# The first loads of a fused matmul-GELU-matmul in smaller pieces

## The chip, the core and the metric

The kernel runs on one core of a Trainium2 chip. The metric is the device time of one execution in microseconds; the median of several runs counts. A profile is one execution recorded by the hardware profiler, with the start and length of each instruction on TensorE (PE; its weight loads PEld), VectorE (DVE), ScalarE (ACT), GpSimd (POOL) and SyncE (SP), and the DMA packets.

## What is computed

```python
def setup_inputs():
    m, k, n, p = 1024, 1024, 2048, 1024
    # a: [m, k], b: [k, n], c: [n, p], all float32, standard normal

def reference(a, b, c):
    h = np.matmul(a, b)
    h = 0.5 * h * (1 + np.tanh(np.sqrt(2 / np.pi) * (h + 0.044715 * h ** 3)))
    return np.matmul(h, c).astype(np.float32)
```

## The kernel before

All matmuls run on 128 x 128 weights against up to 512 columns. The hidden matrix h is made transposed: its 2048 columns are 16 tiles of 128 partitions, and the 1024 rows of A are two halves (h = 0, 1 in the code) of 512. The contraction of the first product has 1024 entries, eight slices of 128 (k = 0 to 7), and pairs of slices are called quarters (q = 0 to 3). A has to lie with the contraction on the partitions, so each 128 x 128 block of it is cast to bf16, transposed on TensorE into a PSUM bank (`pt`) and copied by VectorE into `aT`.

The kernel has three stages in this order:

1. The first four column tiles of h (columns 0 to 511 of B) with plain matmuls: `block(h, tiles, ks)` adds the slices `ks` to the accumulators `ps[h, t]` of the given tiles; `gelu` writes the finished ones into `hT`. In this stage A is turned, slice by slice, in between the blocks.
2. The other column tiles, by a scheme with seven products in place of eight (`zero`, a block of 512 columns, then `one`, the last 1024), with sums and differences of operands made by VectorE.
3. The second product with C (`two`), by the same scheme, with the stores of the result.

The order on every engine is the order in which the program is written (`manual_schedule`); engines wait for each other only through tiles. The order in front is written out by hand: `stir` keeps TensorE busy with products of zeros, `cast_a` and `cast_b` cast what came in float32, `turn` transposes a quarter (two slices, with a `yield` after each), `block` does the matmuls.

Loads take two ways. SyncE's queue brings float32 into staging tiles: `sta` for A (lines 75, 77, 78: quarter 0 of both halves and quarter 1 of half 0, 512 KB each, rows of 256 columns) and `stb` for B (lines 76 and 79: slices 0 and 1 in one load of 512 KB, slice 2 of 256 KB). VectorE and ScalarE cast these. GpSimd's queue, called the casting queue here, casts on the way: `abq` for A (line 86) and straight into `b1`, `b2` and `c_sb` for B and C (lines 89, 92, 98, 101, 104). A one-column copy on GpSimd, `gate` (line 81), stands ahead of the casting loads and waits for the first load of A, so that the casting queue starts only then. The casting loads in order are: A (h=1, q=1), B slice 3, A (0,2), B slices 4 and 5, A (1,2), A (0,3), B slices 6 and 7, A (1,3), then the second column block of B, the last 1024 columns of B, and C.

Which slices of the casting queue arrive when decides what stage 1 can do: `block(0, range(4), (k,))` needs `b1[:, k]` and `aT[:, 0, k]`, and `turn(1, 3, ...)` on the last load of A stands near the end of the stage. After that stage 2 begins with products over the second column block of B.

Of the kernel before, what the change touches and what calls it, by code (L numbers as in the profile page):

```python
# [9 lines left out]
F32 = mybir.dt.float32  # L10
F32R = mybir.dt.float32r
BF16 = mybir.dt.bfloat16
# [7 lines left out]
def kernel(ctx, tc, a, b, c, out):  # L20
    nc = tc.nc
    M, K = a.shape
    _, N = b.shape
    _, P = c.shape
    H = 512
# [3 lines left out]
    av = a.rearrange("(mt p) k -> p mt k", p=128)  # L29
    bv = b.rearrange("(kt p) n -> p kt n", p=128)  # L30
# [9 lines left out]
    def slot(tag, shape, dt, name):  # L40
        return big.tile(shape, dt, name=name, tag=tag)

    def bank(i, shape=(128, H), dt=F32, name="ps"):
        return pp.tile(list(shape), dt, name=name, tag=f"bank{i}", padded_shape=None)

    def pieces(tag, bufs, shape, dt, name):
        return small.tile(shape, dt, name=name, tag=tag, bufs=bufs)

    warm = nc.const_aps.tensor(0.0, [128, 256], F32)
    ident = consts.tile([128, 128], BF16, name="ident")  # L50
    make_identity(nc, ident)
    gate = consts.tile([128, 1], F32, name="gate")
# [6 lines left out]
    aT = slot("a", [128, 2, KT, H], BF16, "aT")  # L59
    b1 = slot("b1", [128, KT, 1024], BF16, "b1")  # L60
# [2 lines left out]

    KH = KT // 2
    stb = slot("x0", [128, KT, H], F32, "stb")
    sta = slot("x1", [128, 2, 2, 4, 256], F32, "sta")
    abq = slot("x3", [128, 4, 2, 4, 256], BF16, "abq")

    def a_part(h, q):
        return av[:, 4 * h:4 * h + 4, ds(q * 256, 256)]  # L70

    def b_part(q):
        return bv[:, 2 * q:2 * q + 2, 0:H]

    nc.sync.dma_start(out=sta[:, 0, 0], in_=a_part(0, 0))
    nc.sync.dma_start(out=stb[:, 0:2], in_=b_part(0))
    nc.sync.dma_start(out=sta[:, 1, 0], in_=a_part(1, 0))
    nc.sync.dma_start(out=sta[:, 0, 1], in_=a_part(0, 1))
    nc.sync.dma_start(out=stb[:, 2], in_=bv[:, 2, 0:H])

    nc.gpsimd.tensor_copy(gate, sta[:, 0, 0, 3, 0:1])  # L81
    nc.scalar.activation(g, warm[:, 0:1], AF.Gelu_apprx_tanh)


    def cast_load_a(h, q):
        nc.gpsimd.dma_start(out=abq[:, q, h], in_=a_part(h, q))  # L86

    def cast_load_b(q):
        nc.gpsimd.dma_start(out=b1[:, 2 * q:2 * q + 2, 0:H], in_=b_part(q))  # L89

    cast_load_a(1, 1)
    nc.gpsimd.dma_start(out=b1[:, 3, 0:H], in_=bv[:, 3, 0:H])  # L92
    for q in range(2, 4):
# [5 lines left out]
    for n in range(2):  # L99
        for k in range(0, KT, 4):  # L100
            nc.gpsimd.dma_start(out=b2[:, k:k + 4, ts(n, H)],
                                in_=bv[:, k:k + 4, ds(1024 + n * H, H)])
# [3 lines left out]
    def copy(eng, dst, src):  # L106
        if eng is nc.scalar:
            nc.scalar.activation(dst, src, AF.Copy)
        else:
            nc.vector.tensor_copy(dst, src)  # L110

    def mm1(p, t, h, ks):
        for k in ks:
            nc.tensor.matmul(p, b1[:, k, ts(t, 128)], aT[:, h, k],  # L114
                             start=(k == 0), stop=(k == KT - 1))
# [6 lines left out]
    def stir(*widths):  # L122

        for w in widths:
            nc.tensor.matmul(ps[0, 3][:, 0:w], warm[:, 0:128], warm[:, 0:w],
                             start=True, stop=True, skip_group_check=True)

    def cast_a(h, q, *engs):

        ab = pieces("ab", 2, [128, 4, 256], BF16, "ab")  # L130
        for i, eng in enumerate(engs):
            w = 256 // len(engs)
            for j, e in enumerate(eng if isinstance(eng, tuple) else (eng,)):
                m = slice(2 * j, 2 * j + 2) if isinstance(eng, tuple) else slice(0, 4)
                copy(e, ab[:, m, ts(i, w)], sta[:, h, q][:, m, ts(i, w)])
        return ab

    def turn(h, q, i, ab):

        banks = i if isinstance(i, tuple) else (i,)  # L140
        pts = [bank(x, (128, 2, H), BF16, "pt") for x in banks]
        for n in range(2):
            pt = pts[n % len(pts)]
            for m in range(4):
                nc.tensor.transpose(pt[:, n, ts(m, 128)], ab[:, m, ts(n, 128)], ident)  # L145
            nc.vector.tensor_copy(aT[:, h, 2 * q + n], pt[:, n])  # L146
            yield

    def cast_b(k, *engs):
        c0 = 0  # L150
        for i, eng in enumerate(engs):
            w = (H - c0) if i == len(engs) - 1 else H // len(engs) // 128 * 128
            copy(eng, b1[:, k, ds(c0, w)], stb[:, k, ds(c0, w)])
            c0 += w

    def block(h, tiles, ks):
        for k in ks:
            for t in tiles:
                mm1(ps[h, t], t, h, (k,))
# [66 lines left out]
    zero = Seven(4, quarters(b1, H, 256), BB, [None] * 4, [None] * 4, 2)  # L226
    one = Seven(4, quarters(b2, 0, H), BB, [None] * 4, zero.t)

    stir(256, 256, 256, 256, 256)
    tn = turn(0, 0, 4, cast_a(0, 0, nc.vector))  # L230
    next(tn)
    stir(128)
    cast_b(0, nc.vector, nc.vector, nc.scalar)
    next(tn)
    stir(64)
    cast_b(1, nc.scalar)
    ab = cast_a(1, 0, nc.vector, nc.scalar)
    block(0, range(4), (0,))
    block(0, range(2), (1,))
    for _ in turn(1, 0, (7, 6), ab):  # L240
        pass
    block(0, range(2, 4), (1,))
    ab = cast_a(0, 1, (nc.scalar, nc.vector), nc.vector)
    cast_b(2, nc.scalar, nc.scalar)
    for t in range(3):
        ps[1, t] = bank(4 + t)
    zero.t[0], zero.t[1] = pair(2)
    block(1, range(3), (0,))
    tn = turn(0, 1, 7, ab)
    next(tn)  # L250
    block(1, range(3), (1,))
    next(tn)
# [1 line left out]
    for q in range(1, 3):  # L254
        k = 2 * q
        block(0, range(4), (k,))
        tn = turn(1, q, 7, abq[:, q, 1])
# [5 lines left out]
        tn = turn(0, q + 1, 7, abq[:, q + 1, 0])  # L263
# [10 lines left out]
    tn = turn(1, 3, 0, abq[:, 3, 1])  # L274
# [213 lines left out]
```

## Time and profile before

| what | us |
|---|---|
| median of 3 runs | 117.2 (117.19 to 117.28) |
| the profiled execution's own time | 117.6 |
| its span, first to last instruction | 115.8 |
| first load of A landed, GpSimd's gate starts | 4.49 |
| first matmul of the first product | 6.90 |
| last casting load of A landed | 21.58 |
| last matmul ended | 112.9 |

Granted TensorE clock 1.000 of full speed. The DMA issues of the front, from the page (line, engine, operation, count, KB each, median us from issue to landing):

```profile
b<-in_b_dram POOLq DMA_DIRECT2D x6, 512.0 KB, 15.6
sta<-in_a_dram SPq DMA_DIRECT2D x3, 512.0 KB, 6.2
abq<-in_a_dram POOLq DMA_DIRECT2D x5, 256.0 KB, 8.0
stb<-in_b_dram SPq DMA_DIRECT2D x1, 512.0 KB, 5.4
b<-in_b_dram POOLq DMA_DIRECT2D x2, 256.0 KB, 8.3
stb<-in_b_dram SPq DMA_DIRECT2D x1, 256.0 KB, 7.2
```

KB are those written: a casting load of A of 256 KB reads 512 KB. The time to landing holds the waiting in line behind earlier loads. A share of the DMA engines over 100% means that packets overlap. In the lines of a timeline the bracket tells how long the engine stood idle before the instruction, and what ended that.

### The profile page before, as it was taken

How to read it: one execution, taken by the hardware profiler on the slowest of the kernel's cores; microseconds unless marked ns; L12 is line 12 of the kernel's file. 1: busy time of each engine (PE TensorE's matmuls, PEld its weight loads, DVE VectorE, ACT ScalarE, POOL GpSimd, SP SyncE). 2: the span in 40 equal slices, each digit the busy share in tenths (PEclk: the TensorE clock that was granted, in tenths of full speed). 3: DMA queues.
4: the chain of work that ended last, by engine and by line, in shares of the span. 5: the costliest groups of instructions: out<-in, count | busy, mean ns of one | idle time of the engine just before them, and what ended most of it. 6: DMA issues, size and time to landing. Idle time of an engine off the chain costs nothing.

```text
span 115.8 us, 1473 instructions
## 1 busy us (share of the span) xinstructions
PE 110.7 (96%) x544; PEld 77.1 (67%) x550; DVE 90.1 (78%) x108; ACT 51.4 (44%) x86; POOL 17.3 (15%) x29
## 2 busy tenths in 40 slices
PE   7889999999999999999999999999999999999990
PEld 6545555445777447888886444588888888888870
DVE  0247747689999998944789999999999986964581
ACT  5053000799268998066699339700043992000000
POOL 2497754222332000000000000000000000000000
PEclk9999999999999999999999999999999999999999
DMA  3999999999999999998000000070000002004994
GB/s 74 296 381 221 200 199 204 204 207 207 205 210 210 211 212 212 212 210 163 9 0 0 6 0 0 0 272 0 0 0 0 0 0 94 2 27 173 364 358 166
DMA packets 13414, 15.94 MB, mean 138 GB/s; under 512 B 736, under 2 KB 9184, under 8 KB 13408
## 3 DMA queue, kind: packets, MB, share of 16 engines
q0 software_dynamic: 8672, 9.31, 47.6%
q1 hardware_dynamic: 4592, 6.42, 15.7%
q10 hardware_dynamic: 144, 0.13, 0.3%
q8 instruction: 4, 0.07, 0.2%
q14 instruction: 2, 0.02, 0.0%
HBM read 20.97 MB, written 4.19 MB: 217 GB/s over the span
## 4 chain that ended last, share of the span: by engine, by line
PE 79%; DMA 13%; POOL 5%; issue 0%; DVE 0%
PE ps L212 76%; DMA abq<-in_a_dram 10%; DMA sta<-in_a_dram 3%; POOL abq L86 3%; PE ps L114 2%; POOL b L89 1%; POOL gate L81 1%; PE pt L145 1%; POOL b L92 0%; DVE ot L375 0%
## 5 line engine op out<-in xcount | busy, mean ns | idle before, releaser
L212 PE MATMUL ps<-x,s 128*128 128x512 f32 x128 | 29.6, 391 | 0.0
L212 PEld LDWEIGHTS ps<-x,s 128*128 128x128 f32 x128 | 24.0, 188 | 5.1
L212 PE MATMUL ps<-x,x 128*128 128x512 f32 x96 | 22.9, 394 | 0.0
L212 PEld LDWEIGHTS ps<-x,x 128*128 128x128 f32 x96 | 18.0, 188 | 3.9
L114 PE MATMUL ps<-aT,b 128*128 128x512 bf16 x62 | 15.7, 379 | 0.3 <-DVE b L110 0.2
L298 ACT ACTIVATE v<-ps 128x512 f32<-128x512 f32 x10 | 6.0, 598 | 19.1 <-PE ps L212 19.1
L212 PE MATMUL ps<-c_sb,hT 128*128 128x512 bf16 (+2 forms) x78 | 14.1, 336 | 0.1
L212 PE MATMUL ps<-x 128*128 128x512 f32 x56 | 13.2, 393 | 0.0
L212 PEld LDWEIGHTS ps<-x 128*128 128x128 f32 x56 | 10.2, 188 | 2.7 <-ACT u L298 0.4
L212 PEld LDWEIGHTS <-hT 128*128 128x128 bf16 x80 | 7.1, 98 | 7.0 <-issue 0.5
L118 ACT ACTIVATE hT<-ps 128x512 bf16<-128x512 f32 x14 | 7.3, 596 | 9.6 <-PE ps L114 9.6
L118 ACT ACTIVATE hT<-ot 128x512 bf16<-128x512 f32 x18 | 10.4, 623 | 2.1 <-DVE ot L303 2.0
L146 DVE COPY aT<-pt 128x512 bf16<-128x512 bf16 x16 | 6.7, 422 | 5.5 <-PE pt L145 5.4
L212 PE MATMUL ps<-aT,b 128*128 128x512 bf16 x46 | 10.6, 379 | 0.1
L303 DVE TENSOR_TENSOR ot<-ps,u 128x512 f32<-128x512 f32 x10 | 6.7, 688 | 5.2 <-ACT u L298 5.2
L303 DVE TENSOR_TENSOR ot<-ps,v 128x512 f32<-128x512 f32 x10 | 6.7, 688 | 4.9 <-DMA out_dram<-ot 3.9
L170 DVE TENSOR_TENSOR x<-c_sb 128x1024 fp32r<-128x1024 bf16 x8 | 9.2, 1216 | 0.0
L114 PEld LDWEIGHTS <-b 128*128 128x128 bf16 x64 | 5.7, 97 | 4.5 <-DVE b L110 0.3
L212 PEld LDWEIGHTS <-b 128*128 128x128 bf16 x48 | 4.6, 97 | 5.7 <-issue 0.3
L104 POOL DMA_DIRECT2D c_sb<-in_c_dram x8 | 5.6, 703 | 13.4 <-DMA b<-in_b_dram 11.1
L170 DVE TENSOR_TENSOR x<-b 128x1024 fp32r<-128x1024 bf16 (+1 forms) x4 | 7.0, 1751 | 0.6 <-issue 0.6
L298 ACT ACTIVATE u<-ps 128x512 f32<-128x512 f32 x10 | 5.9, 597 | 3.4 <-PE ps L212 3.2
(44 smaller groups left out, 110.7 us busy)
## 6 DMA issues: line engine op xcount, KB each, us to landing
c_sb<-in_c_dram POOLq DMA_DIRECT2D x8, 512.0 KB, 19.7
out_dram<-ot SPq DMA_DIRECT2D x14, 256.0 KB, 2.1
b<-in_b_dram POOLq DMA_DIRECT2D x6, 512.0 KB, 15.6
sta<-in_a_dram SPq DMA_DIRECT2D x3, 512.0 KB, 6.2
abq<-in_a_dram POOLq DMA_DIRECT2D x5, 256.0 KB, 8.0
stb<-in_b_dram SPq DMA_DIRECT2D x1, 512.0 KB, 5.4
b<-in_b_dram POOLq DMA_DIRECT2D x2, 256.0 KB, 8.3
stb<-in_b_dram SPq DMA_DIRECT2D x1, 256.0 KB, 7.2
```

The source lines that it names most:

```text
L81: nc.gpsimd.tensor_copy(gate, sta[:, 0, 0, 3, 0:1])
L86: nc.gpsimd.dma_start(out=abq[:, q, h], in_=a_part(h, q))
L89: nc.gpsimd.dma_start(out=b1[:, 2 * q:2 * q + 2, 0:H], in_=b_part(q))
L104: nc.gpsimd.dma_start(out=c_sb[:, t:t + 2], in_=cv[:, t:t + 2])
L114: nc.tensor.matmul(p, b1[:, k, ts(t, 128)], aT[:, h, k], start=(k == 0), stop=(k == KT - 1))
L118: nc.scalar.activation(hT[h][:, t], p, AF.Gelu_apprx_tanh)
L145: nc.tensor.transpose(pt[:, n, ts(m, 128)], ab[:, m, ts(n, 128)], ident)
L146: nc.vector.tensor_copy(aT[:, h, 2 * q + n], pt[:, n])
L170: nc.vector.tensor_tensor(out=dst[:, r], in0=x[:, r], in1=y[:, r], op=op)
L212: nc.tensor.matmul(p[:, ds(c0, w)], l[:, k, ts(j, 128)], r[:, k, ds(c0, w)], start=(start and k == 0), stop=(k == self.kt - 1), skip_group ...
L298: nc.scalar.activation(st, p, AF.Copy)
L303: nc.vector.tensor_tensor(out=ot, in0=p, in1=st, op=ADD)
```

## The change

The loads on SyncE's queue become six of 256 KB, one slice each, alternating between A and B: A (half 0, slice 0), B slice 0, A (1,0), A (0,1), B slice 1, A (1,1). The rows of an A load are 128 columns long and no longer 256. The staging tile has one entry for each (slice, half). A (h=0, q=1) and B slice 2 are loaded by the casting queue, at its head. The gate waits for the first load as before, which is now half as large.

On the engines, quarter 0 of A is cast and turned one slice at a time: `cast_a(h, k, (engine, rows), ...)` splits a slice's four row blocks over engines, `turn_one` transposes one slice of one half, `keep_one` copies it into `aT`; the two slices of one half no longer share a step. `turn(0, 1, 7, ...)` reads the casting queue's `abq[:, 1, 0]`, and the casts of A (0, q=1) and of B slice 2 are gone. The blocks of slices 0 and 1 are interleaved with these steps. From the loop over q = 1, 2 on, the program is the same.

```diff
-    sta = slot("x1", [128, 2, 2, 4, 256], F32, "sta")
+    sta = slot("x1", [128, 8, 4, 128], F32, "sta")
...
-    nc.sync.dma_start(out=sta[:, 0, 0], in_=a_part(0, 0))
-    nc.sync.dma_start(out=stb[:, 0:2], in_=b_part(0))
-    nc.sync.dma_start(out=sta[:, 1, 0], in_=a_part(1, 0))
-    nc.sync.dma_start(out=sta[:, 0, 1], in_=a_part(0, 1))
-    nc.sync.dma_start(out=stb[:, 2], in_=bv[:, 2, 0:H])
-
-    nc.gpsimd.tensor_copy(gate, sta[:, 0, 0, 3, 0:1])
+    def load_a(h, k):
+        nc.sync.dma_start(out=sta[:, 2 * k + h], in_=av[:, 4 * h:4 * h + 4, ts(k, 128)])
+
+    def load_b(eng, k):
+        eng.dma_start(out=stb[:, k], in_=bv[:, k, 0:H])
+
+    load_a(0, 0)
+    load_b(nc.sync, 0)
+    load_a(1, 0)
+    load_a(0, 1)
+    load_b(nc.sync, 1)
+    load_a(1, 1)
+
+    nc.gpsimd.tensor_copy(gate, sta[:, 0, 3, 0:1])
...
+    cast_load_a(0, 1)
+    nc.gpsimd.dma_start(out=b1[:, 2, 0:H], in_=bv[:, 2, 0:H])
     cast_load_a(1, 1)
...
-    def cast_a(h, q, *engs):
-
-        ab = pieces("ab", 2, [128, 4, 256], BF16, "ab")
-        for i, eng in enumerate(engs):
-            w = 256 // len(engs)
-            for j, e in enumerate(eng if isinstance(eng, tuple) else (eng,)):
-                m = slice(2 * j, 2 * j + 2) if isinstance(eng, tuple) else slice(0, 4)
-                copy(e, ab[:, m, ts(i, w)], sta[:, h, q][:, m, ts(i, w)])
-        return ab
+    def cast_a(h, k, *parts):
+
+        m0 = 0
+        for eng, m in parts:
+            r = slice(m0, m0 + m)
+            copy(eng, ab[k][:, h, r], sta[:, 2 * k + h][:, r])
+            m0 += m
+
+    def turn_one(h, k):
+        for m in range(4):
+            nc.tensor.transpose(pt[k][:, h, ts(m, 128)], ab[k][:, h, m], ident)
+
+    def keep_one(h, k):
+        nc.vector.tensor_copy(aT[:, h, k], pt[k][:, h])
...
-    stir(256, 256, 256, 256, 256)
-    tn = turn(0, 0, 4, cast_a(0, 0, nc.vector))
-    next(tn)
+    ab = [pieces("ab", 2, [128, 2, 4, 128], BF16, "ab") for k in range(2)]
+    pt = [bank(6 + k, (128, 2, H), BF16, "pt") for k in range(2)]
+    stir(256, 256, 256, 256, 128)
+    cast_a(0, 0, (nc.vector, 2), (nc.vector, 2))
+    turn_one(0, 0)
+    keep_one(0, 0)
     stir(128)
-    cast_b(0, nc.vector, nc.vector, nc.scalar)
-    next(tn)
+    cast_b(0, nc.scalar, nc.scalar)
     stir(64)
-    cast_b(1, nc.scalar)
-    ab = cast_a(1, 0, nc.vector, nc.scalar)
-    block(0, range(4), (0,))
-    block(0, range(2), (1,))
-    for _ in turn(1, 0, (7, 6), ab):
-        pass
-    block(0, range(2, 4), (1,))
-    ab = cast_a(0, 1, (nc.scalar, nc.vector), nc.vector)
-    cast_b(2, nc.scalar, nc.scalar)
+    cast_a(1, 0, (nc.vector, 2), (nc.scalar, 2))
+    cast_a(0, 1, (nc.vector, 2), (nc.scalar, 2))
+    block(0, range(2), (0,))
+    turn_one(1, 0)
+    keep_one(1, 0)
+    block(0, range(2, 4), (0,))
+    turn_one(0, 1)
+    keep_one(0, 1)
+    cast_b(1, nc.scalar, nc.scalar)
+    cast_a(1, 1, (nc.vector, 2), (nc.scalar, 2))
     for t in range(3):
         ps[1, t] = bank(4 + t)
     zero.t[0], zero.t[1] = pair(2)
     block(1, range(3), (0,))
-    tn = turn(0, 1, 7, ab)
+    block(0, range(2), (1,))
+    turn_one(1, 1)
+    keep_one(1, 1)
+    block(0, range(2, 4), (1,))
+    tn = turn(0, 1, 7, abq[:, 1, 0])
     next(tn)
     block(1, range(3), (1,))
```

## The prediction

> **What bounds the kernel now.** I read the page's shares first, then the chain of waits in order of time, then the timeline around the places where the chain leaves TensorE, and last the DMA view in narrow windows.
>
> ```profile
> span 115.8 us, 1473 instructions
> PE 110.7 (96%) x544; PEld 77.1 (67%) x550; DVE 90.1 (78%) x108; ACT 51.4 (44%) x86; POOL 17.3 (15%) x29
> DMA  3999999999999999998000000070000002004994
> PE ps L212 76%; DMA abq<-in_a_dram 10%; DMA sta<-in_a_dram 3%; POOL abq L86 3%; PE ps L114 2%; POOL b L89 1%; POOL gate L81 1%; PE pt L145 1%; POOL b L92 0%; DVE ot L375 0%
> ```
>
> TensorE fills the end and DMA the beginning. The chain of waits says where the handover is (start, length, what):
>
> ```profile
> 10.15 11.43 DMA abq<-in_a_dram
> 21.58 0.05 issue
> 21.63 0.40 PE pt L145 x4
> ...
> 22.92 1.94 PE ps L114 x9
> 24.87 2.81 PE ps L212 x13
> ...
> 73.79 39.11 PE ps L212 x188
> ```
>
> Nine matmuls in 1.94 us are 0.216 us each, and from 21.63 to 112.9 nothing but TensorE stands in the chain. So the end comes a fixed time after the last load of A (h=1, q=3) lands at 21.58. The timeline shows how much room TensorE has before that:
>
> ```profile
> 4.49 0.70 POOL L81 COPY gate<-sta 128x1 f32<-128x1 f32 x1 [3.19 <-DMA sta<-in_a_dram]
> 5.14 0.88 POOL L86 DMA_DIRECT2D abq<-in_a_dram  x1
> 6.90 1.47 PE L114 MATMUL ps<-aT,b 128*128 128x512 bf16 x6 [0.17 <-DVE b L110]
> 15.16 1.03 PE L114 MATMUL ps<-aT,b 128*128 128x512 bf16 x4
> 16.02 0.39 PE L145 MATMUL pt<-ident,abq 128*128 128x128 bf16 x4
> 19.16 2.32 PE L114 MATMUL ps<-aT,b 128*128 128x512 bf16 x10
> 21.62 0.23 PEld L145 LDWEIGHTS <-abq 128*128 128x128 bf16 x4 [0.64 <-DMA abq<-in_a_dram]
> ```
>
> The ten matmuls at 19.16 end at 19.16 + 10 x 0.216 = 21.32, the transposes after them start at 21.63: TensorE waits 0.3 us for this load. At 15.16 four matmuls end at 16.02, exactly where the next transposes start (their load, h=1 q=2, was issued at 7.97 with 8.0 us to landing, so 15.97). TensorE and the stream of loads therefore run neck and neck from 12 to 22 us. A TensorE that starts earlier gains nothing by itself; it waits for the stream. **What sets the end is when the DMA stream delivers**, and only a TensorE over 0.3 us late at 12 us would replace it.
>
> Now the stream. Loads on SyncE's queue run until about 10 us, then the casting queue alone. DMA windows 6.25 to 8.25 (A loads in 1 KB packets), 114.2 to 114.4 (the last stores, in 512 B packets), 4 to 5.5 (the first B load) and 9.5 to 10.5 (casting queue); packets, MB, share of 16 engines:
>
> ```profile
> DMA packets 771, 0.77 MB, mean 387 GB/s; under 512 B 21, under 2 KB 765, under 8 KB 771
> q1 hardware_dynamic: 771, 0.77, 109.2%
> ...
> DMA packets 112, 0.05 MB, mean 261 GB/s; under 512 B 10, under 2 KB 112, under 8 KB 112
> q1 hardware_dynamic: 112, 0.05, 88.4%
> ...
> DMA packets 193, 0.38 MB, mean 253 GB/s; under 512 B 4, under 2 KB 12, under 8 KB 193
> ...
> q0 software_dynamic: 375, 0.19, 140.9%
> ```
>
> **The change, part by part.** *Bytes.* Up to the load of B's slice 3 both orders read the same: before 2.25 MB on SyncE plus 0.75 MB of casting loads, after 1.5 MB plus 1.5 MB. So nothing is saved in bytes before any later load.
>
> *Two loads moved to the casting queue* (A h=0 q=1, 512 KB; B slice 2, 256 KB). SyncE's queue reads 387 GB/s in the second window. The casting queue writes 199 GB/s (0.19 to 0.20 MB in 1 us) in half-width elements, so it reads 398 GB/s. 786 KB take 2.03 us by the one and 1.98 by the other: 0.0 us. GpSimd issues two more DMAs (0.88 and 0.55 us by the first rows of that kind) ahead of the others. The next eight issues took it from 5.14 to 10.98, and now ten end near 12; their data is wanted from about 8 us to 19, so the issues stay ahead. Cover gone, each would cost its 0.5 to 0.9 us. Three SP issues of about 0.5 us become four of A and two of B; data flows at 0.7 us per 256 KB against an issue every 0.5 us, so the queue isn't starved. The casts that fall away (A h=0 q=1, 1.6 us over ACT and DVE, B slice 2, 0.8 us on ACT) are off the chain: 0.0.
>
> *A's rows in pieces of 128 columns.* Four loads with 512 B packets (2048 packets, 1 MB) stand where 1 KB packets stood. Mean 1 KB packet: 109.2% x 16 x 2.0 us / 750 = 46.6 ns. Mean 512 B packet: 88.4% x 16 x 0.2 us / 102 = 27.7 ns, so half the bytes cost 0.6 of the time. Extra: (2048 x 27.7 - 1024 x 46.6) ns = 9.0 us of engine time, over 17.5 packets in flight (109.2% of 16): +0.5 us. The row is a store, the change makes loads; bounds: 0.0 (a 512 B packet takes exactly half) to +2.7 us (it takes as long as a 1 KB one). I take 0.5, the only row with this packet size.
>
> The Trainium skill ("DMA: Bandwidth & Descriptors", Specifications) gives 512 B and more as enough for line rate. By that rule this term is 0.0; the store row (27.7 against 46.6 ns) says otherwise, and I go by the row.
>
> *A slow stretch.* In 4 to 5.5 us the first B load ran at 253 GB/s, against 387 later: 524 KB took 2.07 us and not 1.37, a loss of 0.7. Whether it belongs to the first touch of B or to that time, the trace doesn't say. With only half of B in the first load, a loss that goes with that load halves (-0.35); one that goes with the time, or with B's first two slices, stays (0.0). I take -0.15. Bounds -0.35 and +0.35 (smaller packets in the same stretch lose more).
>
> *TensorE in front.* First A load: 4.44 - 1.37 (512 KB) + 0.81 (256 KB in small packets) = 3.9. Then at the rates above: B0 4.9, A(1,0) 5.9, A(0,1) 6.7, B1 7.4, A(1,1) 8.2, cast A(0,q1) 9.6, cast B2 10.2, cast A(1,q1) 11.5. The instruction order then gives, with DVE casts of 0.28 us, ACT halves of 0.42, turns of 0.22 and copies of 0.42: first block at 5.4 instead of 6.90; keep_one(1,0) queues behind DVE's cast of A(0,1), which waits until 6.7, so aT h=1 k=0 is there at 7.4 and the blocks behind it run 7.5 to 8.6; turn_one(1,1) 8.7; the q=1 turns 9.6 and 10.5; blocks of k=2 10.7 to 11.6; turn(1,1) at 11.6 where the trace before has it at 12.02. TensorE is 0.4 us ahead there and waits again for the stream: 0.0, and it costs only if it falls 0.7 us behind. What is late next after 21.58 is B's second column block (issued 12.38, 13.8 us to landing: 26.2), which TensorE needs at 24.7 + 8 x 0.216 = 26.4; it shifts with the same stream.
>
> *Sum:* 0.0 + 0.5 - 0.15 + 0.0 = **+0.35 us**. The profiled execution took 117.6 us around its span of 115.8, so it would become 117.95; the median of the runs is 0.4 lower, 117.2, which gives 117.55; I write 117.5.
>
> **The rivals.** *(a) Faster: the slow stretch belongs to the first B load.* Place: 4 to 5.5 us. If 512 B loads cost half a 1 KB one (0.0 instead of 0.5) and the stretch halves (-0.35), the last A load lands at 21.23 and the end moves by 0.35: 116.85. It decides once the extra of the small packets is under 0.35 us less 0.23, some 24 ns a packet. For it: the shorter first load, and TensorE's 0.4 us lead that lets it follow. Against: the 27.7 ns row.
>
> *(b) No difference: the packets' extra and the shorter stretch cancel, or both are nil.* For it: the same bytes through the same engines at the same rate, 387 against 398 GB/s. Time 117.2.
>
> *(c) Slower by more: a hole between the two queues.* Before, the gate opens at 4.44 and the casting queue's first three packets appear in the window 8.7 to 8.9: 4.3 us later. If that is a latency and not waiting for SyncE's queue to drain, the first comes at 3.9 + 4.3 = 8.2 and perhaps 8.5, while SyncE's engines run dry from about 7.7: up to 0.8 us idle, 0.35 + 0.6 gives 118.15. Against: it began just when SyncE's queue ran out, which looks like waiting in line. If the queues should mix instead, B1 and A(1,1) come up to 1.4 us later, TensorE passes 12 us some 0.6 late, and 0.3 is added: 117.85.
>
> *(d) The small packets are limited by count.* SyncE's window made 385 packets per us in both queues' 1 KB reads; at that count for 512 B, 1 MB costs the upper bound, 2.7 us less the 0.15: 119.75.
>
> **How the numbers follow.** Forecast, +0.23 to +0.7: 0.38. (a) 0.19. (b) 0.22. (c), either way, 0.16. (d) 0.05. 0.2% of 117.2 us is 0.23 us, about what this kernel's runs (117.19 to 117.28) tell from no change. Faster is (a), 0.19; same (b), 0.22; slower the rest, 0.59. The likeliest case's own range is 117.4 to 117.9. For 8 in 10 the range reaches down to (a)'s 116.85, and a little past it, 116.8, and up past (c) to 118.6; (d) stays out.
>
> **What would show it.** SyncE's queue: 6 loads, its packets up by 384 data packets from 4592; the casting queue up by 640 from 8672. First block near 5.4 us: the early start is real. The casting queue's first packets right behind SyncE's last, with no hole near 8 us. Packets of 512 B near 28 ns in the window 6 to 8. The last A load near 21.9, with TensorE idle before its transposes again, and the same 91 us behind it. I am wrong if that load lands before 21.5, if it lands after 22.5, or if TensorE comes to its transposes without waiting, for then TensorE and not the stream sets the end.

## The result and the profile after

The changed kernel takes **118.94 us** (median of 4 runs, 118.49 to 119.04) against 117.21 (117.19 to 117.28): a ratio of 1.0139, interval 1.0113 to 1.0165. It is slower, as forecast, but by 1.7 us and not by 0.35, and above the upper end of the range, 118.6. The profiled execution took 118.9 us around a span of 117.1. In some executions a core is in a slower state, over 1.5% above the fastest of the same kernel; medians below hold these, ratios leave them out, and of the profiles only that of e10_bsplit (121.13 us, its other runs 118.29 to 119.81) is of such an execution.

The page of the changed kernel: span, TensorE, the DMA rows in 40 slices of 2.93 us, and the shares of the chain of waits by line.

```profile
span 117.1 us, 1481 instructions
PE 112.0 (96%) x550; PEld 77.6 (66%) x550; DVE 89.2 (76%) x107; ACT 51.3 (44%) x87; POOL 18.1 (15%) x31
...
DMA  3899999999999999998000000070000002014993
GB/s 107 161 321 198 200 198 200 208 207 206 206 207 210 212 213 211 212 209 166 13 0 0 6 0 0 0 269 0 0 0 0 0 0 93 2 63 177 375 358 101
...
PE ps L226 75%; PE ps L123 9%; DMA b<-in_b_dram 6%; DMA sta<-in_a_dram 2%; PE pt L159 2%; POOL abq L93 1%; POOL b L99 0%; POOL gate L88 0%; DVE ot L396 0%
```

The DMA row still says 8 to 9 tenths busy in the second slice, but the row under it says 161 GB/s there; before it was 296. Engines that count as busy carried half the data. The row of tenths hides this, so the next view has three microseconds of both kernels in windows. The last three columns are the granted clock, the DMA share and GB/s. Before:

```profile
3.00:4.00 1.00, 1.00 (x4) 0.78 (x3) 0.00 (x0) 0.00 (x0) 0.00 (x0) 1.00 1.07 351
4.00:5.00 1.00, 0.79 (x4) 0.35 (x2) 0.54 (x1) 0.00 (x0) 0.51 (x1) 1.00 0.97 262
5.00:6.00 1.00, 0.67 (x6) 0.50 (x7) 0.51 (x2) 0.00 (x0) 1.00 (x2) 1.00 0.94 276
```

After:

```profile
3.00:4.00 1.00, 1.00 (x4) 0.77 (x3) 0.49 (x2) 0.00 (x0) 0.55 (x2) 1.00 0.86 104
4.00:5.00 1.00, 1.00 (x7) 0.85 (x6) 0.00 (x0) 0.00 (x0) 1.00 (x2) 1.00 0.78 124
5.00:6.00 1.00, 1.00 (x8) 1.00 (x6) 0.42 (x1) 0.00 (x0) 1.00 (x3) 1.00 1.00 276
```

From 3 to 5 us, 613 has become 228: some 0.38 MB that were not read, a microsecond of stream at 387 GB/s. The DMA view of 3 to 4 us shows what the packets did, first before:

```profile
DMA packets 319, 0.35 MB, mean 351 GB/s; under 512 B 15, under 2 KB 280, under 8 KB 319
...
q1 hardware_dynamic: 319, 0.35, 107.3%
```

and after:

```profile
DMA packets 78, 0.10 MB, mean 104 GB/s; under 512 B 7, under 2 KB 34, under 8 KB 78
...
q1 hardware_dynamic: 78, 0.10, 85.7%
```

A packet took 107.3% x 16 x 1 us / 319 = 54 ns before and 176 ns after. Among the latter are nine of B's first slice that lasted 0.49 to 1.32 us and two of the A load behind it (0.66 and 0.82); these eleven make 9.6 of the 13.7 us of packet time in that window. Before, one packet lasted over 0.5 us (0.51) between 2 and 7 us; after, 17 did. The trace doesn't tell which engine held which packet. This gap is called **the hole** below.

The chain of waits after (start, length, what) no longer rests on the last load of A, but on B's slice 3:

```profile
0.74 2.66 DMA sta<-in_a_dram
...
5.83 7.42 DMA b<-in_b_dram
13.25 0.05 issue
13.29 1.04 PE ps L123 x4
...
25.83 88.00 PE ps L226 x408
113.83 0.02 issue
113.85 0.29 DVE ot L396
```

and the timeline after shows where TensorE waits in front (bracket: idle before, and what ended it):

```profile
6.84 0.60 PE L123 MATMUL ps<-aT,b 128*128 128x512 bf16 x2 [0.60 <-ACT b L117]
10.65 0.23 PEld L159 LDWEIGHTS <-abq 128*128 128x128 bf16 x4 [0.61 <-DMA abq<-in_a_dram]
13.29 0.55 PEld L123 LDWEIGHTS <-b 128*128 128x128 bf16 x4 [0.39 <-DMA b<-in_b_dram]
17.29 0.23 PEld L159 LDWEIGHTS <-abq 128*128 128x128 bf16 x4 [0.53 <-DMA abq<-in_a_dram]
20.45 2.32 PE L123 MATMUL ps<-aT,b 128*128 128x512 bf16 x10
22.60 0.39 PE L159 MATMUL pt<-ident,abq 128*128 128x128 bf16 x4
```

The first matmul stands at 6.84, where it was at 6.90. The last wait is for A (h=1, q=2), landed 17.25; from there TensorE runs through. The last load of A landed at 21.21, and its transposes came at 22.60 without a wait.

**Where the 1.3 us of the two profiled executions lie.** A (1,2) lands 1.30 later (15.95 to 17.25), and its transposes start 1.27 later, because before TensorE came to them 0.07 after the landing. From their start to the first seven-product matmul TensorE took 8.85 us before (16.02 to 24.87) and 8.54 after (17.29 to 25.83): the wait of 0.3 for the last load is gone. The rest of TensorE's work is alike (88.04 and 88.00). From the end of the last matmul to the end of the span it was 2.91 and is 3.30: +0.39. Sum: 1.27 - 0.31 - 0.04 + 0.39 = 1.31, as the spans differ.

The later landing is itself two things. One is the stream: counting the packets by their ends (a casting load reads twice what it writes), 2 MB (of 2^20 bytes) are in 0.86 later and 6 MB 0.70 later. The other is that a load lands with the slowest of its 16 engines. B's slice 3 was in on the first engine at 11.29 and on the last at 11.98; after, at 11.88 and 13.25: the first is 0.6 late, the last 1.27.

```
MB read (2^20 bytes)    0.25   0.5    1     1.5    2     3     4     6
before, at us           3.07   3.86  5.80  7.19  8.56 11.35 13.97 19.27
after, at us            2.80   4.94  6.63  8.05  9.42 12.06 14.69 19.97
difference             -0.27  +1.08 +0.83 +0.86 +0.86 +0.71 +0.72 +0.70
```

All of the loss is made between 0.25 and 0.5 MB, where B's slice 0 is read, and nearly all of it stays.

**The end.** The waits of SyncE's queue (us in total, times, longest), before and after:

```profile
SPq L483 <- DMA out_dram<-ot: 0.7, 2, 0.4
```

```profile
SPq L504 <- DMA out_dram<-ot: 1.2, 1, 1.2
```

At the end SyncE waits for its DMAs' semaphores one after another, in a fixed order. Loads and stores without a cast take eight semaphores in turn. Five loads and 19 stores are 24, so the last store was on the last of the eight, and 0.87 us after its landing (114.95) the span ended. Six loads make 25: the last store (115.81) is on the first semaphore, the other seven waits come behind it, and the span ends 1.32 us after it. The 0.45 between, over seven waits, is 0.06 us each.

### The profile page after: what moved, and what is told of

Read it like the earlier page. It is cut to its first block, busy times and chain, and to the rows that moved or that the text cites. A ratio compares the mean times of both kernels' runs of the same rounds, so it can differ in the third digit from the quotient of the medians.

```text
span 117.1 us, 1481 instructions
## 1 busy us (share of the span) xinstructions
PE 112.0 (96%) x550; PEld 77.6 (66%) x550; DVE 89.2 (76%) x107; ACT 51.3 (44%) x87; POOL 18.1 (15%) x31
## 4 chain that ended last, share of the span: by engine, by line
PE 86%; DMA 9%; POOL 2%; DVE 0%; issue 0%
PE ps L226 75%; PE ps L123 9%; DMA b<-in_b_dram 6%; DMA sta<-in_a_dram 2%; PE pt L159 2%; POOL abq L93 1%; POOL b L99 0%; POOL gate L88 0%; DVE ot L396 0%
## 5 line engine op out<-in xcount | busy, mean ns | idle before, releaser
L123 PE MATMUL ps<-aT,b 128*128 128x512 bf16 x64 | 16.4, 379 | 0.8 <-ACT b L117 0.6
L226 PE MATMUL ps<-aT,b 128*128 128x512 bf16 x48 | 10.7, 379 | 0.0
L160 DVE COPY aT<-pt 128x512 bf16<-128x512 bf16 x12 | 5.1, 423 | 5.4 <-PE pt L159 5.2
```

The source lines that it names most:

```text
L123: nc.tensor.matmul(p, b1[:, k, ts(t, 128)], aT[:, h, k], start=(k == 0), stop=(k == KT - 1))
L226: nc.tensor.matmul(p[:, ds(c0, w)], l[:, k, ts(j, 128)], r[:, k, ds(c0, w)], start=(start and k == 0), stop=(k == self.kt - 1), skip_group ...
```

## The experiments

Landings are the last engine's; "B3" is B's slice 3, and "2 MB at" is when 2 MB had been read. Both are of one profiled execution of each kernel. Ratios are to the kernel before, run beside each one (117.21 to 117.36).

| run | median us | ratio, interval | 2 MB at | B3 landed |
|---|---|---|---|---|
| before | 117.21 | | 8.56 | 11.98 |
| after | 118.94 | 1.0139, 1.0113 to 1.0165 | 9.42 | 13.25 |
| e1_lane | 117.70 | 1.0035, 1.0015 to 1.0055 | 8.55 | 11.81 |
| e12_lane7 | 118.64 | 1.0113, 1.0089 to 1.0138 | 9.79 | 13.48 |
| e2_thin | 120.92 | 1.0286, 1.0241 to 1.0331 | 9.90 | 14.55 |
| e5_wide | 121.00 | 1.0308, 1.0235 to 1.038 | 9.35 | 13.22 |
| e3_touch | 118.80 | 1.013, 1.0089 to 1.0171 | 9.89 | 13.27 |
| e4_bfirst | 120.63 | 1.0276, 1.0238 to 1.0315 | 9.66 | 14.88 |
| e6_unmove | 120.50 | 1.0258, 1.0157 to 1.0359 | 9.61 | 13.30 |
| e7_bact | 120.70 | 1.0288, 1.0226 to 1.0349 | 9.91 | 15.57 |
| e8_before_bact | 120.20 | 1.0208, 1.0126 to 1.029 | 8.55 | 12.91 |
| e9_rows | 120.39 | 1.0269, 1.0235 to 1.0304 | 9.36 | 13.91 |
| e10_bsplit | 119.08 | 1.0124, 1.0073 to 1.0176 | 9.31 | 13.88 |
| e11_bigA | 120.05 | 1.0218, 1.0186 to 1.025 | 9.27 | 14.95 |
| e14_swap | 118.78 | 1.0119, 1.0038 to 1.02 | 8.52 | 11.82 |
| e13_b_from_a | 119.21 | 1.0156, 1.009 to 1.0221 | 9.71 | 13.69 |
| e15_bsplit_from_a | 118.77 | 1.0118, 1.0035 to 1.0201 | 9.07 | 13.36 |
| e16_big | 119.67 | 1.0185, 1.0149 to 1.0222 | 8.98 | 14.28 |
| e17_big_lane | 119.82 | 1.0211, 1.0184 to 1.0237 | 8.61 | 13.49 |

### The end: one more DMA, or seven

Before, with one DMA of 8 KB more, issued behind the first gelus, where nothing waits for it:

```diff
+    nc.sync.dma_start(out=room, in_=hT[0][:, 0, 0:32])
```

> Kernel before, with one more DMA of 8 KB on SyncE's queue in the middle (near 22 us), where the queue is idle. Theory of the tail: SyncE's closing waits go through the DMA semaphores in a fixed order, 0.06 us each; before, the last store sits on the last of eight semaphores, one DMA more puts it on the first, and seven waits follow its landing: +0.4 us, 117.6. Rival: the 0.4 us between the last store's landing and the end in the changed kernel is chance: 117.2.

The front is that of the kernel before, and the time rises by 0.4 us. Its waits on SyncE's queue:

```profile
SPq L485 <- DMA out_dram<-ot: 1.3, 1, 1.3
```

One long wait in place of two short ones, as in the changed kernel, and 1.32 us from the last store's landing (114.63) to the end. The other direction: after, with seven such DMAs, 6 + 7 + 19 = 32 = 4 x 8.

> Changed kernel, with seven DMAs of 8 KB on SyncE's queue near 23 us, where it is idle, which puts the last store on the second of eight semaphores again, only one of the rest ahead in the waiting order less: 0.06 us less than the changed kernel, 118.9, if the order of SyncE's closing waits is the semaphores' order. A last store far back in that order would give 118.5.

The text on record counts wrongly where it puts the last store on the second semaphore; 32 puts it on the last, and its other figure applies. It came out so: 118.64, and

```profile
SPq L506 <- DMA out_dram<-ot: 0.7, 2, 0.5
```

with 0.89 us from the last store to the end, though this run's hole was the deeper one (2 MB at 9.79). So 0.3 to 0.4 of the 1.7 us are the place of the last store in the order of eight, and have nothing to do with the loads' data.

### The size of the packets

Before, with each of the two 512 KB loads of A's quarter 0 in two column halves (512 B packets):

```diff
-    nc.sync.dma_start(out=sta[:, 0, 0], in_=a_part(0, 0))
+    for k in range(2):
+        nc.sync.dma_start(out=sta[:, 0, 0][:, :, ts(k, 128)], in_=av[:, 0:4, ts(k, 128)])
```

> Kernel before, with A's two loads of quarter 0 cut into column halves (four loads of 256 KB in 512 B packets), all else in the old order, no load moved. Theory P (small packets open the hole of 3 to 5.5 us in SyncE's queue): the hole is as deep as in the changed kernel, the last casting load of A or the one before it lands 1 us later or more, 118.4 or more with 0.35 of the tail. Theory B (the first read of B is slow): the hole stays as before, the extra of the packets alone, 0.3 to 0.5, and the tail 0.35: 117.9. Theory T (the time from 3 to 5.5 us is slow whatever is loaded): as B, 117.9.

Slower by 3.4 us, far more than any price of the packets. After, with A's four loads cut by rows in place of columns, so that the loads stay 256 KB and the packets are 1 KB:

```diff
-        nc.sync.dma_start(out=sta[:, 2 * k + h], in_=av[:, 4 * h:4 * h + 4, ts(k, 128)])
+        nc.sync.dma_start(out=sta[:, h, m:m + 2], in_=av[:, 4 * h + m:4 * h + m + 2, 0:256])
```

> Changed kernel, with A's four loads of 256 KB cut by rows (two row blocks of 256 columns, 1 KB packets) and not by columns; same sizes, same number of loads, B slice 0 still second. Theory P (A's 512 B packets deepen the hole around B's first load): SyncE's queue is done near 8.2 and not 9.3, the casting load of B slice 3 lands near 12.2 and not 13.25, 117.9. Rival Q (the smaller loads in alternation do it, whatever their packets): 13.2 again, 118.9.

```profile
3.00:4.00 1.00, 1.00 (x4) 0.78 (x3) 0.11 (x1) 0.00 (x0) 0.08 (x1) 1.00 0.96 152
4.00:5.00 1.00, 1.00 (x6) 0.75 (x4) 0.19 (x1) 0.00 (x0) 1.00 (x2) 1.00 0.94 154
```

The hole is there without any 512 B packet (the windows of this run: 152 and 154 GB/s), and 2 MB are in at 9.35 against 9.42. Packet size is not the cause. (Its total of 121.0 isn't a price of 1 KB packets: a slice is turned only when both row halves are in, TensorE waits 2.20 us for that, and runs 3.41 us at half its clock behind it.)

### The time, or the first touch of B

After, with an 8 KB read of the same 128 rows of B from ScalarE's queue ahead of everything:

```diff
+    nc.scalar.dma_start(out=room, in_=bv[:, 0, 0:16])
```

> Changed kernel, with an 8 KB read of B's first 128 rows issued by ScalarE's queue at the start, beside the first load of A. Theory B (first read of B's rows is slow): the small read takes the delay on itself, B slice 0 lands near 5 us and not 6.35, and the casting stream comes 1 us earlier: 118.0. Theories P and T: B slice 0 lands at 6.3 again, 118.9.

The read takes the first 64 bytes of each row. B's slice 0 landed at 6.29 (6.35 without): no help. After, with that slice loaded first:

```diff
-    load_a(0, 0)
     load_b(nc.sync, 0)
+    load_a(0, 0)
```

> Changed kernel, with B slice 0 loaded ahead of A's first load. Theory B: the slow stretch moves to the front, to 2 to 4 us, while B is read, and A's loads run at full rate from then on. Theory T: B lands by 3.4 and A's loads run into a hole from 3 to 5.5. Theory P: the hole opens when A's small packets follow. In time: 118.9 or more by each, since the first A load, and the gate with it, is later by 0.7; the trace tells.

```profile
2.00:3.00 1.00, 1.00 (x3) 0.77 (x3) 0.00 (x0) 0.21 (x2) 0.00 (x0) 1.00 0.52 142
3.00:4.00 1.00, 1.00 (x4) 0.78 (x3) 0.00 (x0) 0.00 (x0) 0.00 (x0) 1.00 0.62 146
4.00:5.00 1.00, 0.95 (x4) 0.57 (x2) 0.00 (x0) 0.09 (x1) 0.00 (x0) 1.00 1.02 291
```

The slow stretch goes with B's slice, to 2 to 4 us: it doesn't belong to that time of the kernel. It looks different here: the engines are busy for only 0.52 and 0.62 of the time, and only three packets last over 0.5 us. The 120.63 us aren't its price alone, for at 10 to 12 us the casting queue falls to 62 and 67 GB/s. A's loads come unbroken behind it, so this run also prices the small packets in loads. Its DMA view from 4.5 to 6 us:

```profile
DMA packets 986, 0.50 MB, mean 332 GB/s; under 512 B 29, under 2 KB 981, under 8 KB 986
...
q1 hardware_dynamic: 986, 0.50, 111.3%
```

111.3% x 16 x 1.5 us / 986 = 27.1 ns a packet; the prediction had 27.7 from stores. The Trainium skill ("DMA: Bandwidth & Descriptors", Specifications) puts 512 B at line rate; here it is 332 GB/s, and 1 KB packets of the same rows made 387.

### The queues

After, with A (0, q=1) and B's slice 2 back on SyncE's queue and cast by the engines:

```diff
+    nc.sync.dma_start(out=sta[:, 2], in_=a_part(0, 1))
+    load_b(nc.sync, 2)
...
-    cast_load_a(0, 1)
-    nc.gpsimd.dma_start(out=b1[:, 2, 0:H], in_=bv[:, 2, 0:H])
```

> Changed kernel, with A (h=0, q=1) and B slice 2 back on SyncE's queue behind the six small loads, cast by ScalarE and VectorE; the small pieces stay. Both theories P and Q: the hole opens before these loads, B slice 3 lands near 13.2 again, 118.9 less 0.06 of the tail. Rival M (the move to the casting queue costs the time): B slice 3 near 12.2, 117.8.

The hole is the same (114 and 135 GB/s in 3 to 4 and 4 to 5 us). A (0, q=1) landed at 11.73 (9.37 before), because the casting queue's packets ran among SyncE's from 8.5 us on. So the two moved loads didn't make the hole, and undoing the move alone makes it slower still. After, with B's slices 0 and 1 on ScalarE's queue, and before with its one load of both on that queue:

```diff
-    load_b(nc.sync, 0)
+    load_b(nc.scalar, 0)
...
-    nc.sync.dma_start(out=stb[:, 0:2], in_=b_part(0))
+    nc.scalar.dma_start(out=stb[:, 0:2], in_=b_part(0))
```

> Changed kernel, with B's two float32 loads on ScalarE's queue and not between A's on SyncE's. If the hole is engines standing idle because the loads of one queue are handed out in order and those behind B's slow packets are not handed out yet (theory P), A's loads go on while B's stall: all engines busy from 2 to 6 us, B slice 3 near 12.4, 118.0. If B's packets hold the engines themselves: 13.2 again, 118.9.

> Kernel before, with its first B load (512 KB) on ScalarE's queue. By the same two readings: the slow stretch of 4 to 5.5 us goes and the casting stream comes up to 0.5 us earlier, 116.8; or it stays, 117.2.

Neither helps. On two queues the loads share the engines, and the first load of A lands at 6.02 and 6.36 in place of 3.40 and 4.44; both runs show a stall later, in the casting loads. In e8 2 MB are in as early as before, but the casting queue falls to 84 GB/s in 11 to 12 us, and 4 MB are in 1.10 late (15.07). Its profiled execution took 118.75 us, 1.15 over that of the kernel before. The other three took 120.18 to 120.38 at a mean clock of 0.983 to 0.985, so about half of e8's 3 us stands only in runs at a lower clock.

### The size of the loads

Before, with one thing cut each time. A's quarter 0 by rows (1 KB packets, four loads of 256 KB); B's first load in two:

```diff
-    nc.sync.dma_start(out=sta[:, 0, 0], in_=a_part(0, 0))
+    for m in range(0, 4, 2):
+        nc.sync.dma_start(out=sta[:, 0, 0, m:m + 2], in_=av[:, m:m + 2, 0:256])
...
-    nc.sync.dma_start(out=stb[:, 0:2], in_=b_part(0))
+    for k in range(2):
+        nc.sync.dma_start(out=stb[:, k], in_=bv[:, k, 0:H])
```

> Kernel before, with A's two loads of quarter 0 cut by rows into 256 KB each, still in 1 KB packets; B's first load whole, order as before. Theory R (loads of A of 256 KB on SyncE's queue, whatever their packets, deepen the hole): 2 MB are in 0.8 us or more later than before, B slice 3 lands at 12.8 or later, 118.3 or more with 0.37 of the tail. Rival P (it takes 512 B packets): the hole stays as before, 117.6 by the tail alone.

> Kernel before, with B's first load cut into its two slices of 256 KB. Theory R: no deeper hole, B slice 3 at 12.0, 117.6 by the tail alone. Rival S (any more and smaller loads in front do it): B slice 3 at 12.8 or later, 118.3 or more.

After, with A's quarter 0 in two loads of 512 KB and B's slices 0 and 1 still in 256 KB loads:

> Changed kernel, with A's quarter 0 loaded as before in two loads of 512 KB (order A half 0, B slice 0, A half 1, B slice 1); the engines' order, the casts by slice and the two moved loads stay. Theory R: the hole is as shallow as in the kernel before, B slice 3 near 12.0, 117.3 with 0.06 of the tail. Rival S or M: 13 or later, 118.3 or more.

The stretch of 4 to 5 us in e9, e10 and e11, in this order:

```profile
4.00:5.00 1.00, 1.00 (x4) 0.57 (x2) 0.14 (x1) 0.00 (x0) 0.18 (x2) 1.00 0.72 122
...
4.00:5.00 1.00, 0.82 (x4) 0.39 (x2) 0.23 (x1) 0.00 (x0) 0.20 (x1) 1.00 0.91 112
...
4.00:5.00 1.00, 0.58 (x4) 0.36 (x2) 0.30 (x2) 0.00 (x0) 0.27 (x2) 1.00 0.74 173
```

Either cut is enough: 2 MB are in 0.7 to 0.8 late in all three, where e1, with the loads of before, has them at 8.55. e10's trace is of its execution of 121.13 us; for the cut of B alone, e11's small loads of B and the next section's e15 say the same. A shift of order alone, with the sizes of before (the third and fourth load exchanged), tells whether any disturbance does it:

> Kernel before, with the third and the fourth load (A half 1 quarter 0, A half 0 quarter 1, both 512 KB) in the other order. A control: same sizes, same first two loads. Theory S (smaller loads deepen the hole): 2 MB in near 8.55 as before; TensorE gets A's half 1 up to 1.4 us later, 117.2 to 118. Rival F (the old order is one lucky arrangement, any other one opens the hole): 2 MB near 9.3.

```profile
3.00:4.00 1.00, 1.00 (x4) 0.77 (x3) 0.00 (x0) 0.00 (x0) 0.00 (x0) 1.00 1.12 373
4.00:5.00 1.00, 1.00 (x4) 0.57 (x2) 0.69 (x1) 0.00 (x0) 0.66 (x2) 1.00 0.92 231
```

It doesn't: no packet over 0.4 us, 2 MB at 8.52, B3 at 11.82. (Its 1.5 us are TensorE's, which gets A's other half at 9.25.)

### What is read

After, with the second load taking other columns of A in place of B's slice 0; and e10 with its two loads reading columns of A. Both compute another result and serve for the time alone.

```diff
-    load_b(nc.sync, 0)
+    nc.sync.dma_start(out=stb[:, 0], in_=av[:, 0, H:])
```

> Changed kernel, with the second load (B slice 0) reading the same shape, 128 rows of 2 KB, out of A (rows 0 to 127, columns 512 to 1023) into the same place; the result is then not the reference's. Theory B (reading B for the first time is slow): no hole from 3 to 5.5 us, 2 MB are in near 8.8 and not 9.42, the second load lands near 4.5 and not 6.35, about 118. Rival W (2 KB packets, or the place they are written to, make the hole): the load lands near 6.3 again.

> Kernel before, with the first load of B cut into two of 256 KB as in the run with B split, both reading A's columns 512 to 1023 (rows 0 to 255) and not B; the result is not the reference's. Theory B: no hole, 2 MB in near 8.2, against 9.31 in the run with B split. Rival W: near 9.3 again.

In e13 that load lands at 4.22, not 6.35, without the long packets; but 3 to 5 us still runs at 264 and 190 GB/s and a second hole follows where B's slice 1 is read (218 and 222 GB/s in 6 to 8 us). In e15, which reads no B there, 4 to 6 us makes 135 and 196. Packets of SyncE's queue over 0.5 us in 2 to 9 us are 17 in the changed kernel and none in e13, 13 in e10 and 3 in e15. So reading B takes part in the long packets, but isn't needed for a hole.

### All sizes undone

After, with the three 512 KB loads of before; the two moved loads and the changed order on the engines stay. And the same with two DMAs of 8 KB:

```diff
-    load_a(0, 0)
-    load_b(nc.sync, 0)
-    load_a(1, 0)
-    load_a(0, 1)
-    load_b(nc.sync, 1)
-    load_a(1, 1)
+    load_a(0)
+    nc.sync.dma_start(out=stb[:, 0:2], in_=b_part(0))
+    load_a(1)
```

> Changed kernel, with the three loads of 512 KB that the kernel before starts with (A half 0, B slices 0 and 1, A half 1, each whole); the two loads stay moved, the engines' order and the casts by slice stay. Theory S (a load under 512 KB in front of SyncE's queue opens the hole): 2 MB are in near 8.55, B slice 3 lands near 12.0, and the kernel takes what the kernel before takes: 117.2 to 117.5 with 0.12 of the tail. Rival: the moved loads or the engines' order cost something too, 118 or more.

> The same, with two DMAs of 8 KB on SyncE's queue near 22 us, so that the last store is on the last of the eight semaphores as in the kernel before: 0.12 less than e16, 117.1 to 117.4.

```profile
3.00:4.00 1.00, 1.00 (x4) 0.78 (x3) 0.00 (x0) 0.00 (x0) 0.00 (x0) 1.00 1.06 368
4.00:5.00 1.00, 1.00 (x6) 0.70 (x5) 0.49 (x2) 0.00 (x0) 0.52 (x2) 1.00 1.00 344
...
9.00:10.00 1.00, 1.00 (x6) 0.55 (x5) 0.41 (x1) 0.41 (x2) 1.00 (x2) 0.50 0.93 77
```

In e16's windows the hole on SyncE's queue is gone: 368 and 344 GB/s, 1.5 MB at 7.09 (7.19 before, 8.05 after). Yet a new one opens at 8.75 to 10.5 us (77 GB/s in 9 to 10), in the casting queue, where B's slice 2 now is read, and B3 lands at 14.28. The same in e17, so the two 8 KB DMAs can't be read off there. TensorE was also late here, at half its clock in the profiled execution (the last section shows it), but e16's executions at a clock of 0.995 to 1.000 took 118.62 to 119.68 too, and the kernel is no faster than the changed one. So the size of the loads opens the hole on SyncE's queue, but it isn't the whole price of the change: with big loads, the casting queue stalls instead. That the moved loads cause this isn't shown: e8 moves none and its casting queue stalls too, while the changed kernel moves both and its casting queue doesn't. No run beat the kernel before.

## Why the prediction was right and wrong

**Right: the stream bounds the front, TensorE doesn't.** The chain goes from loads to TensorE and then stays there. TensorE was ready before B's slice 3 and A (1,2), and A (1,2)'s delay passed on.

**Right: the bytes (0.0) and the time of a small packet. Not shown: that the kernel pays it.** 400 packets more on SyncE's queue (384 predicted, of data) and 672 on the casting queue (640). A 512 B load packet takes 27.1 ns. By the prediction's own working that is (2048 x 27.1 - 1024 x 46.6) ns / 17.8 = 0.44 us for the **+0.5**. Whether the kernel pays it can't be told: 0.5 to 1.5 MB, with three of the four such loads, took 3.11 us, 337 GB/s, but with 1 KB packets (e5) it took 3.21, and 2 MB came only 0.07 sooner. The term explains none of the excess.

**Wrong: the slow stretch, "-0.15, bounds -0.35 and +0.35".** This is the step that failed. The stretch was seen in the trace of before, and the question was asked rightly, whether it belongs to B or to the time. But it was costed as a loss that would shrink or stay with the size of the load. With smaller loads it grew: in place of -0.15 the stream lost 1.08 us at 0.5 MB, 0.86 at 2 MB and 0.70 at 6 MB. e9, e10 and e11 show that halving A's two loads does this, or halving B's, e5 that small packets aren't needed.

**Wrong with it: landings from mean rates.** The predicted list (1.5 MB at 8.2, 2 MB at 9.6) is about when the bytes were in (8.05 and 9.42), yet the loads landed at 9.30 and 10.60. Before, the landing of the load that ends with 1.5 MB came 0.78 after its bytes (7.19, 7.97); after, 1.25 (8.05, 9.30). The working took each row's rate as if all 16 engines went together. The 0.47 between is engines out of step, and it stayed to the last casting load. That is also why the first block didn't start at 5.4: by then half a megabyte was in, but B's slice 0 was complete on its last engine at 6.35.

**Missed: the end, +0.39.** The sum counted SyncE's loads (five become six) but gave the count itself no price. e1 gives it one (+0.4), and in e12 it comes off again (-0.3).

**Misread: the last load of A as the releaser.** The trace of before has it landing at 21.58; in e1 and e14, whose streams are as early, it lands at 19.76 and 19.77 and TensorE doesn't wait for it. So "the same 91 us behind it" rested on one odd landing in one execution: its first engine was in at 19.24, its last 2.3 us later. In the changed kernel this load landed at 21.21 and TensorE came to it without waiting, two of the signs that the prediction named for being wrong. Yet the stream still set the end, through an earlier load, A (1,2). A packet of the instruction queue, 16 KB in 3.8% x 16 x 1.6 us = 0.97 us, lies in that window of before (19.0 to 20.6 us):

```profile
q0 software_dynamic: 361, 0.32, 122.9%
q8 instruction: 1, 0.02, 3.8%
```

Two other traces support that it held this engine. The same packet stands at 19.65 us in e1 and at 20.86 in e14, 0.97 us long, and there the next load to land (the first of B's second block) has its last engine 1.01 and 0.87 us behind the last but one, where A's last load had 0.09 and 0.14. The trace names no packet's engine, so it stays argued. It would also explain part of why the medians differ by 1.73 and the profiled executions by 1.3: without the odd wait of 0.31 the spans would differ by 1.62.

**The rivals.** (a) and (b) fall: nothing shrank. (c) was right that the stream would have a hole, but not where or of what kind: it opened at 3 to 5 us inside SyncE's queue, with the engines at shares of 0.86 and 0.78, mostly in long packets. Its 4.3 us from the gate to the first casting packet is no latency: in e4 the gate came at 5.70 and the first casting packet at 7.53. (d) falls by the 27.1 ns.

**Open: what the long packets, and the idle engines of e4, wait for.** Not the time, not the first touch of the rows' first 64 bytes, not the packet size, not the moved loads, not one queue rather than another, and neither B alone nor load size alone. Nor is it shown what opens the casting queue's holes. The Trainium skill ("DMA: Bandwidth & Descriptors", Latency and other measured facts) has a memory access at 0.2 us on average and 2 us at high load. Packets of 0.5 to 1.3 us lie between; no run here shows why the load would be high there.

## What to carry to other kernels

Cost a smaller load by when its last engine lands, not by bytes over a mean rate; and where the trace shows a stretch that runs below the rate around it, take the stretch as able to grow as well as to shrink when the loads in it change. Before resting a sum on one load's landing, look whether its first and last engine agree, for one late engine may belong to that execution alone. Count the DMAs to the end of the kernel: here one more cost 0.4 us by moving the last store in the order of the closing waits.

## What the runs showed of the hardware

**Half clock in front.** In the profiled executions of e16, e17, e5, e7 and e10 TensorE's granted clock fell to 0.50 for 3.41 us, after waits of 0.9 to 2.2 us; in the 3.41 us ahead of the fall TensorE was busy 1.41 to 1.81 us. That doesn't decide it: e6 (10.61 to 14.02 us) and e2 (7.46 to 10.87) were busy 1.50 and 1.69 us in as long a stretch, after waits of 2.3 and 2.4 us, and kept 1.00. The windows of e16 from 8.4 us:

```profile
8.40:11.80 3.40, 3.40 (x15) 1.72 (x16) 1.13 (x4) 1.01 (x4) 2.68 (x4) 0.50 1.11 120
```

The chain of e16 has five matmuls in 1.92 us there, 0.38 each, against 0.216. The kernel before and the changed one keep 1.00 throughout the front.

**Engines out of step stay so.** A spread of 1.3 to 1.4 us between a load's first and last engine at 9 us was still 1.4 at 18.5.

**The queues.** In e6 SyncE's and the casting queue both moved data from 8.5 to 12 us (533 and 598 packets). Neither the issue nor the gate says when a casting load's data starts: 4.3 us after the gate before, 1.8 in e4.
